# Eight value tiles of a two-layer trunk move into paired products, and the last projection leads with two tiles

## The chip, the cores and the metric

The kernel runs on one NeuronCore of one Trainium2 chip. The metric is the device time in microseconds of one execution. Three runs of the kernel before gave 2314.68, 2317.88 and 2318.4 us.

## The reference, cut to what matters

The reference is one inference step of a two-layer trunk over 512 sample tokens and 128 prompt tokens (640 columns, NT) with model width 2048. Layer 1, the odd one, has two mixers. Mixer C is differential attention: four heads, each with two query and two key maps of width 128 and one value of width 256. Mixer D is plain grouped attention with eight query heads and two key/value heads.

```python
cq, ck, cv, cg, dq, dk, dv, dg = split_cols(h @ w_in, ODD_SPLIT)
cv = cv.reshape(b, t, C_HEADS, C_V_DIM).transpose(0, 2, 1, 3)
...
o1 = attend(cq[:, 0][:, :, None], ck_all[:, 0], cv_all)[:, :, 0]
o2 = attend(cq[:, 1][:, :, None], ck_all[:, 1], cv_all)[:, :, 0]
o_c = rms_norm(o1 - lam.astype(o1.dtype) * o2, c_on) * (1.0 - lam_init)
y_c = o_c.transpose(0, 2, 1, 3).reshape(b, t, C_W) * jax.nn.silu(cg)
```

The branch outputs go through one output projection `w_out` and are added, gated, to the input of the layer. The gates of the conditioning come from `silu(c) @ ada_w`. The values of the prompt tokens are also an output (`new_c_v`).

## The kernel before, in words

**Tiles and products.** All activations lie with the 2048 features on 16 row blocks (k) of 128 partitions, 640 token columns each, and every one is split into a high and a low part (`split`, L240: ScalarE writes the high part, VectorE the difference), and so is every 128x512 quarter of weights (`split_w`, L260). A product is three matmuls: high by high, high by low, low by high. One output tile of 128 columns takes 16 blocks x 2 token halves of 320 x 3 = 96 matmuls (`proj_q`, L269). Weights come from DRAM over SP's queue into four `raw` buffers, up to five quarters ahead.

**Single tiles and pairs.** `run_tiles` (L312) computes tiles one by one, four quarters each. After each quarter `slot` (L301) advances the generators that wait in `prep` (the work on a finished tile, such as norms and transposes) and in `attn` (attention, one call per step) and the filler. Some first tiles, the leads, are computed together while their inputs are being made, so that each input serves several tiles. `run_pairs` (L435) computes two tiles from seven products instead of eight, each over 8 row blocks and one half of the tokens, with sums of weights made by VectorE (L467 to L477) and sums of activations made by `forms` (L1061). `project` (L1114) strings these together: three leads, singles up to n0, then pairs.

**Order.** The program's text gives the order in which work is emitted. The framework then orders instructions on each engine, so matmuls of attention can stand in the middle of a projection's quarter. Each engine, and SP's and GpSimd's DMA queues, work in the order so fixed.

**Layer 1's stages.** First the gates (L1430): 14 gate tiles, six as singles and eight as four pairs; each goes to DRAM (`gate_out`, L1396). Then the pool of buffers "mid" is closed, "odd" opened, and 38 single tiles run (L1484): for D query, key and value tiles (`q_gen` L625, `k_gen` L578, `v_gen` L672), then for each C head two query, two key and two value tiles, at the end two late gates (`very_late_gate`, L1445). `v_gen` copies the tile out of PSUM (`stage`, L554), transposes it to token rows in five blocks (`to_rows`, L560), splits it into `vh` and `vl`, and appends the attention of the head to `attn`. `diff_gen` (L1316) is the attention of one C head in 13 calls; `k_gen` drains `attn` before it overwrites a key buffer (L612). Between these runs the conditioning of layer 1 on VectorE (`ada_on_dve`, L191): four blocks of 32 steps of two products each (L213) and one closing step, at a rate FILL1 per quarter from quarter FILL1_FROM on.

**The end.** After the tiles `prep` and `attn` are drained (L1486, L1487), and layer 1's output projection begins with three leads whose inputs `y1_maker` (L1490) loads from DRAM in the order of quarters 0, 2, 3, 1: four tiles of a quarter through buffers "P" (L1502) or, in the other two quarters, three buffers "xr" (`late_yin`, L1102). At the ninth input the pool "odd" is closed and "fin" opened. The third lead accumulates in the PSUM tile that otherwise holds attention scores (`new_pp`, L280).

Of the kernel before, what the change touches and what calls it, by code (L numbers as in the profile page):

```python
# [11 lines left out]
F32 = mybir.dt.float32  # L12
# [36 lines left out]
FILL1 = 1.0  # L49
FILL1_FROM = 16  # L50
# [3 lines left out]
def trunk_kernel(ctx: ExitStack, tc: tile.TileContext, I: dict, O: dict):  # L54
# [523 lines left out]
    def k_gen(ap, pp, tag, src, gain, new_out):  # L578
        raw = ap.tile([P, 2, P], F32, tag="ctxk", name="ctxk", bufs=1)
        nc.sync.dma_start(raw, src.rearrange("(c p) d -> p c d", p=P))  # L580
        x = stage(ap, pp)
        yield
# [3 lines left out]
        for sample in (True, False):  # L586
# [35 lines left out]
        split(hi[:, CTX + NS:CTX + NT], lo[:, CTX + NS:CTX + NT], t)  # L622

# [48 lines left out]
    def v_gen(ap, pp, src, new_out, w=P, j=0, then=None):  # L672
        x = stage(ap, pp)
        yield
        if j == 0:
            drain(attn)
            st["v"] = tuple(ap.tile([P, 7, w], F32R, tag=t, name=t) for t in ("vh", "vl"))
            ctx_v(ap, src, *st["v"], w)
        hi, lo = st["v"]
        cols = slice(j * P, (j + 1) * P)  # L680
        t = to_rows(cols_of(x), True)
        split(hi[:, 2:6, cols], lo[:, 2:6, cols], t.rearrange("p (b f) -> p b f", b=4))
# [3 lines left out]
        split(hi[:, 6, cols], lo[:, 6, cols], vp)  # L686
# [144 lines left out]
    xdram, hdram, gdram = ([dram.tile([P, NT], F32, name=f"{n}{k}") for k in range(KT)] for n in ("xd", "hd", "gd"))  # L831
# [95 lines left out]
    def k_job(tag, src, gain, new_out):  # L927
        return lambda pp: k_gen(pools["cur"], pp, tag, src, gains[gain], new_out)
# [185 lines left out]
    def project(w, cols, n0, maker, job, begin, part, done, tail, **kw):  # L1114

        go_on = run_tiles([(cols[n], job(n)) for n in range(3)], w, maker, **{"order": (0, 2, 1, 3), **kw})


        quarters = [(cols[n], qd) for n in range(3, n0) for qd in range(4)]
# [10 lines left out]
        for n in range(3, n0):  # L1130
            pp, t = new_pp((n - 3) % 2), 4 * (n - 3)
# [298 lines left out]
    project(I["od_w_in"][0], [(OD["cg"] + i * P) if i < 8 else OD["dg"] + (i - 8) * P for i in FRONT], N_FRONT, h1_maker,  # L1430
# [31 lines left out]
    for n in range(4):  # L1462
# [4 lines left out]
        if n % 2 == 0:  # L1467
            jobs.append((OD["dk"] + kv * P, k_job(f"k{kv}", I["cache_d_k"][0, 0, kv], "d_k_norm", O["new_d_k"][0, 0, kv])))
            jobs.append((OD["dv"] + kv * P, v_job(I["cache_d_v"][0, 0, kv], O["new_d_v"][0, 0, kv], P, 0, then)))
# [116 lines left out]
```

## Time and profile before

| | |
|---|---|
| median of three runs | 2317.88 us (2314.68 to 2318.4) |
| profiled execution | 2318.59 us |
| its span, first to last instruction | 2316.8 us |
| mean granted TensorE clock | 0.997 |
| busy: TensorE, VectorE, ScalarE, GpSimd | 98%, 71%, 42%, 8% of the span |
| matmuls | 15892 |
| DMA | 342.94 MB, 148 GB/s over the span |

Layer 1's pairs run from about 1215 to 1317 us of the span, the odd stage to about 2088, the leads of the last projection to about 2137. The profile lists for each engine its busy time, for groups of instructions the count and mean duration and what ended the idle time before them, and in the windows view the busy time of each engine within a stretch. A matmul's listed duration includes its way through the array and overlaps the next one.

### The profile page before, as it was taken

What the parts mean: (1) busy time and instruction counts of PE and PEld (TensorE: products, weight loads), DVE (VectorE), ACT (ScalarE), POOL (GpSimd) and SP (SyncE); (2) the same over time, 40 slices, a digit from 0 to 9 for tenths busy, and PEclk for the clock granted to TensorE, in tenths of its full rate; (3) what the DMA queues carried; (4) which work ended last, traced back from release to release, by engine and by line L of the source; (5) the groups of instructions that cost most, each with busy time, mean ns of one, the idle gap of its engine ahead of it and who ended that gap; (6) DMA issues with size and microseconds to landing.
All of it is one profiled execution on the core that took longest, in us unless ns stands there. A gap on an engine that the chain in (4) does not pass through costs nothing.

```text
span 2316.8 us, 41604 instructions
## 1 busy us (share of the span) xinstructions
PE 2272.1 (98%) x15892; PEld 2197.3 (95%) x15892; DVE 1635.5 (71%) x3308; ACT 969.7 (42%) x2007; POOL 175.6 (8%) x243
## 2 busy tenths in 40 slices
PE   7999999999999999999999999999999999999999
PEld 5699999999999999999999999999999999999999
DVE  4559886786866663988887658659657658557576
ACT  4335442433422222544644445555453444434343
POOL 2111000000000000000100000000001010100101
PEclk9999999999999999999999999999999999999999
DMA  9874545445455543844773433224315233318532
GB/s 364 330 260 130 154 124 163 144 122 165 121 180 160 152 139 114 283 140 127 242 223 107 135 102 97 63 81 131 97 52 153 66 92 113 92 60 281 176 119 70
DMA packets 388456, 342.94 MB, mean 148 GB/s; under 512 B 19298, under 2 KB 327024, under 8 KB 387744
## 3 DMA queue, kind: packets, MB, share of 16 engines
q1 hardware_dynamic: 376000, 294.35, 41.9%
q0 software_dynamic: 11536, 43.77, 5.0%
q8 instruction: 125, 2.05, 0.4%
q10 hardware_dynamic: 720, 2.16, 0.3%
q14 instruction: 75, 0.61, 0.1%
HBM read 301.93 MB, written 38.28 MB: 147 GB/s over the span
## 4 chain that ended last, share of the span: by engine, by line
PE 86%; DVE 4%; ACT 3%; DMA 3%; issue 2%; POOL 1%; SPq 0%; ACTq 0%; POOLq 0%; DVEq 0%
PE pa L276 9%; PE pb L277 9%; PE pb L276 9%; PE pa L277 9%; PE pb L278 9%; PE pa L278 9%; PE pq L535 5%; PE pq L537 5%; PE pq L536 5%; PE T L715 2%; PE T L178 1%; PE S L727 1%; PE S L729 1%; PE S L728 1%; DMA yin<-yd 1%
## 5 line engine op out<-in xcount | busy, mean ns | idle before, releaser
L241 ACT ACTIVATE wh<-raw 128x512 fp32r<-128x512 f32 (+1 forms) x466 | 288.4, 619 | 723.8 <-PE pb L277 615.4
L276 PE MATMUL pa<-h,wh 128*128 128x320 f32 x1632 | 519.2, 319 | 4.8 <-ACT h L908 2.5
L242 DVE TENSOR_TENSOR wl<-raw,wh 128x512 fp32r<-128x512 f32 (+1 forms) x466 | 313.8, 674 | 296.3 <-ACT wh L241 260.9
L277 PE MATMUL pa<-h,wh 128*128 128x320 f32 x1632 | 508.3, 312 | 2.8 <-DVE h L242 2.7
L278 PE MATMUL pa<-h,wl 128*128 128x320 f32 x1632 | 506.9, 311 | 0.0
L278 PE MATMUL pb<-h,wl 128*128 128x320 f32 x1632 | 505.5, 310 | 0.0
L276 PE MATMUL pb<-h,wh 128*128 128x320 f32 x1632 | 505.2, 310 | 0.0
L277 PE MATMUL pb<-h,wh 128*128 128x320 f32 x1632 | 505.0, 309 | 0.0
L213 DVE SCALAR_TENSOR_TENSOR acc<-adaw,sT,acc 128x512 f32<-128x512 f32 (+1 forms) x600 | 358.3, 636 | 14.0 <-DMA adaw<-in_ada_w 13.7
L276 PEld LDWEIGHTS pa<-h,wh 128*128 128x128 f32 x1632 | 307.9, 189 | 18.2 <-issue 9.3
L277 PEld LDWEIGHTS pa<-h,wh 128*128 128x128 f32 x1632 | 308.4, 189 | 7.3 <-DVE h L242 4.5
L278 PEld LDWEIGHTS pa<-h,wl 128*128 128x128 f32 x1632 | 307.9, 189 | 3.3 <-issue 3.3
L278 PEld LDWEIGHTS pb<-h,wl 128*128 128x128 f32 x1632 | 306.6, 188 | 2.1 <-issue 2.1
L276 PEld LDWEIGHTS pb<-h,wh 128*128 128x128 f32 x1632 | 306.7, 188 | 0.0
L277 PEld LDWEIGHTS pb<-h,wh 128*128 128x128 f32 x1632 | 306.5, 188 | 0.1
L535 PE MATMUL pq<-h,wh 128*128 128x320 f32 x480 | 149.7, 312 | 0.4 <-DVE xr L1099 0.2
L536 PE MATMUL pq<-h,wh 128*128 128x320 f32 x480 | 148.4, 309 | 0.0
L537 PE MATMUL pq<-h,wl 128*128 128x320 f32 x480 | 148.0, 309 | 0.0
L701 ACT ACTIVATE p<-S,nm,rq 128x768 f32<-128x768 f32 (+3 forms) x120 | 101.2, 843 | 101.4 <-DVE nm L696 67.1
L535 PE MATMUL pq<-T,wh 128*128 128x320 f32 x360 | 111.2, 309 | 0.0
L536 PE MATMUL pq<-T,wh 128*128 128x320 f32 x360 | 111.2, 309 | 0.0
L537 PE MATMUL pq<-T,wl 128*128 128x320 f32 x360 | 111.2, 309 | 0.0
(326 smaller groups left out, 3699.8 us busy)
## 6 DMA issues: line engine op xcount, KB each, us to landing
adaw<-in_ada_w SPq DMA_DIRECT2D x192, 256.0 KB, 3.0
raw<-in_ev_w_in SPq DMA_DIRECT2D x184, 256.0 KB, 3.0
raw<-in_od_w_in SPq DMA_DIRECT2D x184, 256.0 KB, 2.9
ada<-in_ada_w SPq DMA_DIRECT2D x14, 2048.0 KB, 10.5
adaw<-in_ada_w SPq DMA_DIRECT2D x128, 128.0 KB, 2.2
yd<-y POOLq DMA_DIRECT2D x32, 320.0 KB, 3.0
yin<-yd SPq DMA_DIRECT2D x32, 320.0 KB, 4.4
w<-yd SPq DMA_DIRECT2D x32, 320.0 KB, 4.1
```

Source lines behind the costliest of these rows:

```text
L178: PE.matmul(acc[32 * g:32 * g + 32, 0:wd], sT[:, kt, :], w[:, kt % m, :], start=(i < 4), stop=(i >= KT - 4), tile_position=(0, 32 * g))
L213: V.scalar_tensor_tensor(out=a, in0=w, scalar=sT[:, kt, c:c + 1], in1=a, op0=ALU.mult, op1=ALU.add)
L241: A.activation(hi, x, AF.Copy)
L242: V.tensor_sub(lo, x, hi)
L276: PE.matmul(ps, wh[:, i, :], hi[:, sl], start=(j == js[0] if alone else (pos == 0 and j == 0)), stop=False)
L277: PE.matmul(ps, wh[:, i, :], lo[:, sl], start=False, stop=False)
L278: PE.matmul(ps, wl[:, i, :], hi[:, sl], start=False, stop=(j == js[1] - 1 if alone else (pos == 3 and j == 3)))
L535: PE.matmul(ps, wh[:, j, :], hi, start=(h == 0 and j == 0), stop=False)
L536: PE.matmul(ps, wh[:, j, :], lo, start=False, stop=False)
L537: PE.matmul(ps, wl[:, j, :], hi, start=False, stop=(h == 1 and j == 3))
L701: A.activation(p[:, 0:n], s, AF.Exp, scale=rsc, bias=nm, accum_out=l)
L715: PE.transpose(t[:, i * P:(i + 1) * P], p, ident)
```

## The change

The eight value tiles of mixer C leave the single tiles of the odd stage and follow the gates as four more pairs. `value_out` copies a finished half into the tile that the gates use for their tanh; `value_rows` transposes the finished tile to token rows, copies them, stores them to DRAM (`vdram`) and stores the prompt rows to the output. The first key tile of each head (`k_gen` with `vals`) loads its two value tiles back through buffers "stg" and splits them into `vh` and `vl`; the second one (`then`) appends the head's attention. In the odd stage the conditioning runs at 1.25 steps per quarter from the first quarter on, and attention at 1.1 calls per quarter from the fourteenth tile on. The drain of `attn` ahead of the last projection goes; that projection takes two leads instead of three (`n_lead`), and its inputs of the quarters 0 and 2 come through buffers "rp" and "stg" instead of "P".

```diff
-FILL1 = 1.0
-FILL1_FROM = 16
+FILL1 = 1.25
+FILL1_FROM = 0
...
-    def k_gen(ap, pp, tag, src, gain, new_out):
+    def k_gen(ap, pp, tag, src, gain, new_out, vals=None, then=None):
+        vx = []
+        def v_in(j):
+            vx.append(ap.tile([P, 5, P], F32, tag="stg", name="vx", bufs=2))
+            nc.sync.dma_start(vx[j].rearrange("p b f -> p (b f)"), vals[1][j])
...
         x = stage(ap, pp)
+        if vals:
+            v_in(0)
         yield
...
+        if vals:
+            v_in(1)
...
         split(hi[:, CTX + NS:CTX + NT], lo[:, CTX + NS:CTX + NT], t)
+        if vals:
+            yield
+            hi, lo = st["v"] = tuple(ap.tile([P, 7, 2 * P], F32R, tag=t, name=t) for t in ("vh", "vl"))
+            ctx_v(ap, vals[0], hi, lo, 2 * P)
+            for j in range(2):
+                cols = slice(j * P, (j + 1) * P)
+                split(hi[:, 2:7, cols], lo[:, 2:7, cols], vx[j])
+        if then:
+            attn.append(then())
...
-    def project(w, cols, n0, maker, job, begin, part, done, tail, **kw):
-        go_on = run_tiles([(cols[n], job(n)) for n in range(3)], w, maker, **{"order": (0, 2, 1, 3), **kw})
-        quarters = [(cols[n], qd) for n in range(3, n0) for qd in range(4)]
+    def project(w, cols, n0, maker, job, begin, part, done, tail, n_lead=3, **kw):
+        go_on = run_tiles([(cols[n], job(n)) for n in range(n_lead)], w, maker, **{"order": (0, 2, 1, 3), **kw})
+        quarters = [(cols[n], qd) for n in range(n_lead, n0) for qd in range(4)]
...
+    def value_rows(n, t):
+        yield
+        r = pools["cur"].tile([P, 5, P], F32, tag="xr", name="vr", bufs=3)
+        A.copy(r[:, 0:4, :], to_rows(cols_of(st[t]), True).rearrange("p (b f) -> p b f", b=4))
+        A.copy(r[:, 4, :], to_rows(cols_of(st[t]), False))
+        nc.gpsimd.dma_start(vdram[n], r.rearrange("p b f -> p (b f)"))
+        nc.gpsimd.dma_start(O["new_c_v"][0, 0, n // 2][:, n % 2 * P:(n % 2 + 1) * P], r[:, 4, :])
+    def value_out(n):
+        def put(t, sl, src):
+            A.copy(st[t][:, sl], src)
+            if (n, "v") in half_done:
+                prep.append(value_rows(n, t))
+            half_done.add((n, "v"))
+        return put
...
     def front_begin(p):
         for t in range(2):
-            outs[t] = gate_out(N_FRONT + 2 * p + t)
+            n = N_FRONT + 2 * p + t
+            outs[t] = gate_out(n) if n < len(FRONT) else value_out(n - len(FRONT))
...
-    project(I["od_w_in"][0], [(OD["cg"] + i * P) if i < 8 else OD["dg"] + (i - 8) * P for i in FRONT], N_FRONT, h1_maker,
+    project(I["od_w_in"][0], [(OD["cg"] + i * P) if i < 8 else OD["dg"] + (i - 8) * P for i in FRONT]
+            + [OD["cv"] + i * P for i in range(8)], N_FRONT, h1_maker,
             front_job, front_begin, None, front_done, front_tail, by_half=True)
...
         for m in range(2):
+            more = (None, diff_then(h)) if m else ((I["cache_c_v"][0, 0, h], vdram[2 * h:2 * h + 2]),)
             jobs.append((OD["ck"] + (m * 4 + h) * P,
-                         k_job(f"k{m}", I["cache_c_k"][0, 0, m, h], "c_k_norm", O["new_c_k"][0, 0, m, h])))
-        for j in range(2):
-            jobs.append((OD["cv"] + h * 256 + j * P,
-                         v_job(I["cache_c_v"][0, 0, h], O["new_c_v"][0, 0, h][:, j * P:(j + 1) * P], 256, j,
-                               diff_then(h) if j else None)))
-    brisk = {len(jobs), len(jobs) + 1}
+                         k_job(f"k{m}", I["cache_c_k"][0, 0, m, h], "c_k_norm", O["new_c_k"][0, 0, m, h], *more)))
+    brisk = {len(jobs): 1.5, len(jobs) + 1: 1.5}
+    brisk.update((i, 1.1) for i in range(13, len(jobs)))
...
     drain(prep)
-    drain(attn)
...
-            t = pools["cur"].tile([P, 768], F32, tag="P", name="yin", bufs=P_BUFS)[:, 0:NT]
+            tag, n = (("rp", 3), ("stg", 2))[k % 2]
+            t = pools["cur"].tile([P, NT], F32, tag=tag, name="yin", bufs=n)
...
-    project_out(1, y1_maker, rows_out, rows_last, lambda name: None, order=(0, 2, 3, 1))
+    project_out(1, y1_maker, rows_out, rows_last, lambda name: None, n_lead=2, order=(0, 2, 3, 1))
```

More of the change, by code (lines that the diff above doesn't have):

```diff
@@ L670, in ctx_v, with v_gen @@
         split(hi[:, 0:2, :], lo[:, 0:2, :], raw)
-    def v_gen(ap, pp, src, new_out, w=P, j=0, then=None):
+    def v_gen(ap, pp, src, new_out, then=None):
         x = stage(ap, pp)
         yield
-        if j == 0:
-            drain(attn)
[L677 to L680, printed above, removed]
+        drain(attn)
+        hi, lo = st["v"] = tuple(ap.tile([P, 7, P], F32R, tag=t, name=t) for t in ("vh", "vl"))
+        ctx_v(ap, src, hi, lo, P)
         t = to_rows(cols_of(x), True)
-        split(hi[:, 2:6, cols], lo[:, 2:6, cols], t.rearrange("p (b f) -> p b f", b=4))
+        split(hi[:, 2:6, :], lo[:, 2:6, :], t.rearrange("p (b f) -> p b f", b=4))
         t = to_rows(cols_of(x), False)
@@ L1129, in project @@
         go_on()
[L1130 to L1131 removed]
+        for n in range(n_lead, n0):
+            pp, t = new_pp((n - n_lead) % 2), 4 * (n - n_lead)
             for hv in ([HV] if n < n0 - 1 else [HV[1:], HV[:1]]):
```

14 lines of the change are left out of this document (7 added, 7 removed).

## The prediction

> **What bounds the kernel now.** I read the busy line of the page first, then the windows view by stage, then the groups of the stages that the change touches, and last the waits around two joins.
>
> ```profile
> span 2316.8 us, 41604 instructions
> ...
> PE 2272.1 (98%) x15892; PEld 2197.3 (95%) x15892; DVE 1635.5 (71%) x3308; ACT 969.7 (42%) x2007; POOL 175.6 (8%) x243
> ```
>
> TensorE (PE) is busy for 2272.1 of 2316.8 us, so all its idle time together is 44.7 us: a change gains by taking matmuls away, and loses by opening gaps. In the windows the first number after the stretch is its length, then come the busy time and instruction count of PE, weight loads, DVE, ACT and POOL, the granted clock, the DMA share and GB/s.
>
> ```profile
> 1215.00:1317.00 102.00, 102.00 (x696) 101.80 (x696) 77.30 (x128) 47.85 (x86) 4.41 (x9) 1.00 0.33 103
> 1317.00:1655.00 338.00, 334.95 (x2370) 324.80 (x2369) 239.36 (x537) 172.03 (x364) 26.10 (x27) 1.00 0.33 99
> 1655.00:2088.00 433.00, 424.24 (x2958) 412.60 (x2957) 276.39 (x637) 190.60 (x456) 42.06 (x54) 1.00 0.31 93
> 2089.00:2137.00 48.00, 45.21 (x300) 43.55 (x299) 37.80 (x68) 23.54 (x37) 2.77 (x4) 1.00 0.88 283
> ```
>
> The rows are: the gates' four pairs; the odd stage while mixer D's attention runs, and while mixer C's does; and the three leading tiles of layer 1's output projection. The pairs have no PE gap at all; D's stretch idles 3.0 us, C's 8.8, the lead 2.8. A matmul's listed 310 ns overlaps its neighbour, so its price is the distance between starts:
>
> ```profile
> 1240.10 0.31 PE L536 MATMUL pq<-h,wh 128*128 128x320 f32 x1
> ...
> 1241.42 0.31 PE L536 MATMUL pq<-h,wh 128*128 128x320 f32 x1
> ```
>
> These starts are nine matmuls and 1.32 us apart, and 102.00 us over 696 gives the same: **146.6 ns each**.
>
> **The change, part by part.**
>
> *Matmuls.* A single tile takes 16 row blocks x 2 halves x 3 products = 96 matmuls, two tiles 192. A pair takes 7 products of 8 x 3 = 24, so 168. Eight value tiles lose 768 from the C stage and put 672 into the front: 96 fewer, 96 x 146.6 ns = **-14.1 us**. The five transposes of a value tile move from its single tile to value_rows, count unchanged: nothing, between -0.5 and +1.
>
> *The load of a value pair on DVE and ACT.* Two single tiles need 8 weight splits, a pair 14, and the adds on top. (Groups: line, engine, operation, tiles, count, then busy us and mean ns of one, then the idle time before and its releaser.)
>
> ```profile
> L242 DVE TENSOR_TENSOR wl<-sx,wh 128x512 fp32r<-128x512 f32 x24 | 16.5, 688 | 12.2 <-ACT wh L241 12.2
> L470 DVE TENSOR_TENSOR sx<-sx,w 128x1024 f32<-128x1024 f32 x4 | 4.9, 1226 | 0.1
> L1400 DVE SCALAR_TENSOR_TENSOR g<-sq,tables 128x320 f32<-128x320 f32 x8 | 3.9, 487 | 0.0
> ```
>
> In the gates' pairs DVE has 77.30 us in 102.00, or 18.6 us in the 24.6 us that 168 matmuls take. A value pair replaces four gate products of 0.487 us by copies on ACT, so DVE falls to about 16.7 us. ACT, at 47.85 us there, gets four copies and two row copies in place of four tanh. PE hides all this as it does today: nothing. If that cover were gone a pair would last as long as its DVE work, which is still shorter. POOL issues two DMAs per tile instead of one; in that stage it is busy 4.41 of 102 us and nothing urgent queues behind them.
>
> *The end of the front.* The last value tile's transposes stand behind the last product, its add and its copy, and the front now ends by draining them, with the odd stage's first matmuls behind them on PE. An operation on 128x320 is 0.49 us (last row above) and the copy is near that, so the chain costs between 0 (PE gets odd-stage matmuls first) and 2.5 us. I take **+1**, two such operations.
>
> *Mixers D and C with fewer quarters.* The odd stage falls from 152 quarters to 120. By their matmuls the stretches hold:
>
> ```profile
> L276 PE MATMUL pa<-h,wh 128*128 128x320 f32 x352 | 112.5, 320 | 0.0
> L213 DVE SCALAR_TENSOR_TENSOR acc<-adaw,sT,acc 128x256 f32<-128x256 f32 x23 | 9.5, 479 | 0.5 <-DMA adaw<-in_ada_w 0.5
> ```
>
> The first row is one of six such groups of C's stretch: 2112 matmuls, 22 tiles, 88 quarters, so D's stretch has 64; all 32 quarters that go are C's. The conditioning needs 132 steps (four blocks of 33), each two of the second row. Before, it starts after 16 quarters and D takes 48; at 1.25 from the first quarter D takes 80, and C's 52 end well inside its 56 quarters. So 32 x 0.96 = 31 us of DVE move from C to D: D rises from 239.4 to 270 of 338 us (80%), C falls to 276.4 - 31 - 32 splits x 0.69 = 223 us in 433 - 768 x 0.1466 = 320 us (70%). The pairs run without a gap at 76%.
>
> The attention gets denser. One head of C is 13 calls. It enters in the third quarter of the next head's first tile and must be done by the third quarter of its second key tile: 12 quarters x 1.1 = 13.2 calls, so it just fits and the drain ahead of the key finds at most one. The waits that hurt C today are these:
>
> ```profile
> L1368 PE MATMUL T<-ident,on 128*128 128x128 f32 x36 | 7.5, 291 | 5.4 <-DVE on L1362 4.7 <-DVE kg L591 0.3
> L564 PE MATMUL T<-ident,m 128*128 128x128 f32 x28 | 4.9, 300 | 2.6 <-DVE m L609 2.4
> 2039.00:2089.00 50.00, 48.85 (x341) 46.46 (x340) 33.10 (x80) 21.38 (x49) 3.35 (x6) 1.00 0.23 69
> ```
>
> 8.0 us over four heads. The last row is the stretch that already runs 1.5 calls per quarter: it idles 1.15 of 50 us, 2.3%; 2.3% of 320 is 7.4 us, not more than today's 8.8. Against that stands the denser conditioning in D. Bounds: -3 (waits shrink with the stage) and +8 (they double). I take **+1**.
>
> Two value loads per head join SP's queue. They wait for stg buffers, the second one for the key tile's transposes; weight loads and the cache load queue behind them. Weights are loaded up to five quarters, 5 x 24 x 0.1466 = 17.6 us, ahead: nothing, and the same +8 if the cover goes.
>
> *The lead of the last projection.* Three leading tiles become two, the drain ahead of them goes, and the last head's calls 10 to 13 run inside the lead. PE's work there: 192 x 0.1466 = 28.1 us, and about 40 attention matmuls. In C, the 2958 - 2112 = 846 other matmuls share 424.24 - 2112 x 0.1466 = 115 us, 0.136 us each, so 5.4 us. Together 33.5 us, in which all 16 input tiles must be loaded and split.
>
> ```profile
> L241 ACT ACTIVATE h<-yin x16: 718/738/742, 2089.5 to 2126.0; 128x640 fp32r<-128x640 f32 x16
> DMA to landing us min/median/max: 2.7/4.3/6.1
> 2093.34 0.81 DVE L1455 TENSOR_TENSOR gg<-yg,gg 128x640 f32<-128x640 f32 x1
> ```
>
> Before, the 16 splits run from 2089.5 to 2126.0, 36.5 us, while PE has 48 us. The new buffers are tighter: the third and fourth input take buffers that the last gate (L1445) holds until its product, which today is over at 2094.15, some 5 us into the lead, and SP is held behind them. A load then takes 4.3 us to land. At the old pace the last input is split after 36.5 us and its 12 matmuls end about 1.8 us later: 38.3 us, 4.8 us idle where it was 2.8: +2. The early hold can add a short stall, so I take **+3**, between -2.8 (no idle left) and +21 (worked out below). That the third tile becomes a single one costs nothing: its 96 matmuls move.
>
> A longer stall costs more than its length:
>
> ```profile
> PE T L564 <- DVE m L609: 3.6, 4, 2.1
> 1778.00:1784.00 6.00, 4.79 (x34) 4.55 (x32) 4.91 (x12) 1.54 (x3) 1.88 (x2) 1.00 0.38 107
> 1784.00:1788.00 4.00, 3.09 (x13) 3.05 (x14) 3.57 (x8) 0.60 (x1) 0.00 (x0) 0.63 0.54 163
> 1788.00:1792.00 4.00, 4.00 (x28) 4.00 (x27) 2.94 (x8) 1.65 (x4) 0.00 (x0) 0.95 0.47 131
> ```
>
> In the waits (total, times, longest) the longest of this group is 2.1 us: 1.21 idle before 1784 and 0.91 after it. The stretch in which it ends has a clock of 0.63 and holds 13 matmuls where the next holds 28, so it loses 15 x 0.1466 = 2.2 us: 0.91 by idling, 1.3 by the clock.
>
> By the Trainium skill ("TensorE: Matmul & The Clock Gate", section "What's actually happening") the clock goes to half after at least one idle window of about 3.4 us and comes back after about 3.4 us of sustained work. The row differs: here a wait of 2.1 us was enough. By the page's figure no stall that I expect reaches the gate, and the lead's +3 would stay as it is; by the row a single 2 us stall makes it 3 + 1.3 = +4.3.
>
> *Sum.* -14.1 + 1 + 1 + 3 = -9.1 us. The profiled execution took 2318.59 us (span 2316.8), 0.7 above the median of 2317.88. 2318.6 - 9.1 = **2309.5 us**.
>
> **The rivals.**
>
> *Full gain.* The lead fills its waits with attention and gate work, and C keeps fewer waits as it shortens: -14.1 and up to -1 more, 2303 to 2305. For it: 1.5 calls per quarter cost only 2.3% idle. Against it: 33.5 us of PE work against 36.5 us of splits.
>
> *Starved in every quarter, clock falling.* Each of the lead's four quarters waits 2 us for its inputs and loses 1.3 us more to the clock: 13.2 us where 2.8 idle now, +10.4; with +2 elsewhere 2318.6 - 14.1 + 12.4 = 2316.9, no difference. For it: the 2.1 us stall above, and the DMA share of 0.88 with three tiles. Against it: three 320 KB loads overlap today, 36.5 / 16 = 2.3 us apart. The Trainium skill's page named above would give this case only for waits of about 3.4 us.
>
> *Loads one at a time (slower).* If SP, held by each buffer in turn, never has two inputs in flight, the 14 inputs behind the first two come 4.3 us apart: 60 us against 33.5 of work, 26.7 idle for 2.8, and with some overlap of the last ones +21: 2318.6 - 14.1 + 2 + 21 = 2327.5. It decides once the lead loses 16.0 us more than today, with the loads some 3.7 us apart ((33.5 + 2.8 + 16.0) / 14). The three buffers of the later eight inputs speak against it.
>
> *It doesn't do what it says.* The value pairs run slower than PE's pace and eat the 3.5 us that each should save: about 2318. The pairs' row, 102.00 of 102.00, speaks against it.
>
> **How the numbers follow.** About 0.2%, 4.6 us, is what a measurement of this kernel can tell from no change: faster is below 2313.2, slower above 2322.5. Forecast, 2305 to 2313.2: 0.50. Full gain: 0.20. Starved: 0.17. Not as it says: 0.03. Slower: 0.10. So faster 0.70, same 0.20, slower 0.10. The range 2303 to 2320 takes in the full gain and most of the starved case; what it leaves out is the slower rival and the edges, under 0.2.
>
> **What would show it.** PE should run 15796 matmuls: 224 more in each of the pairs' three lines, 256 fewer in each of the single tiles' three. The value pairs should last 24.6 us each without a PE gap; C's stretch about 320 us with some 8 us idle; the lead about 38 us with 4 to 6 us idle, waiting for yin. A lead over 50 us or at a clock below 1.00, more than 16 us idle in C, or value pairs longer than 25 us would make the forecast wrong.

## The result: slower by 0.3%, and the profile after

The changed kernel takes 2324.39 us (median of 7 runs, 2321.26 to 2327.76), the kernel before beside it 2316.97 us (7 runs, 2314.68 to 2319.36). The ratio is 1.0032 (95% interval 1.0020 to 1.0043), where 0.996 was forecast. The profiled execution took 2321.26 us, the shortest of the seven, so it shows somewhat less of the loss than the median does.

The busy line and four stretches of the changed kernel: the eight pairs, D's stretch, C's, the lead of the last projection; the fifth is a piece of the lead.

```profile
span 2319.5 us, 41525 instructions
...
PE 2259.1 (97%) x15796; PEld 2182.4 (94%) x15796; DVE 1678.2 (72%) x3364; ACT 991.9 (43%) x2043; POOL 184.0 (8%) x251
```

```profile
1213.00:1414.00 201.00, 201.00 (x1380) 200.76 (x1379) 144.75 (x229) 95.26 (x174) 11.50 (x22) 1.00 0.34 107
1414.00:1752.00 338.00, 332.64 (x2349) 322.34 (x2348) 255.80 (x586) 170.45 (x362) 28.59 (x28) 0.99 0.37 111
1752.00:2075.00 323.00, 311.30 (x2171) 298.62 (x2171) 229.69 (x527) 163.61 (x402) 39.46 (x46) 1.00 0.31 95
2075.00:2127.00 52.00, 37.85 (x241) 35.25 (x241) 35.74 (x71) 22.07 (x40) 4.51 (x6) 0.93 0.67 219
2104.00:2108.00 4.00, 2.83 (x10) 2.71 (x11) 2.85 (x5) 2.21 (x3) 0.00 (x0) 0.50 0.75 272
```

The 96 matmuls are gone and the pairs have no gap, as forecast. D's stretch idles 5.4 us (3.0 before), C's 11.7 (8.8 before). The lead idles 14.2 of 52.0 us, and its clock is 0.93. The waits of TensorE within the lead, then the groups of the input tiles and SP's issues from 2086 to 2106 (start, duration, queue, line, count):

```profile
PE pa L276 <- ACT h L241: 12.6, 4, 8.4
PE T L564 <- DVE xr L1117: 1.3, 1, 1.3
```

```profile
L241 ACT ACTIVATE h<-yin x16: 722/736/742, 2072.9 to 2121.4; 128x640 fp32r<-128x640 f32 x16
...
DMA to landing us min/median/max: 2.8/4.9/6.6
```

```profile
2088.67 9.58 SPq L254 DMA_DIRECT2D raw<-in_od_w_out  x4
2098.34 1.49 SPq L1122 DMA_DIRECT2D yin<-yd  x3
```

```profile
2096.41 0.38 PE L1386 MATMUL T<-ident,on 128*128 128x128 f32 x2
2105.17 0.64 PE L276 MATMUL pa<-h,wh 128*128 128x320 f32 x1 [8.37 <-ACT h L241]
2105.60 0.47 PE L276 MATMUL pb<-h,wh 128*128 128x320 f32 x1
2105.87 0.47 PE L276 MATMUL pa<-h,wh 128*128 128x320 f32 x1
```

Read them together. From 2088.67 on SP issues four weight loads that belong to the first *single* tile; each waits for a raw buffer, and they hold the queue for 9.58 us. Input 12 stands behind them: its load goes at 2098.34, and TensorE waits 8.37 us for its split. The 16 splits then take from 2072.9 to 2121.4, 48.5 us instead of 36.5.

All kernels below are divided in the same way, into five pieces of the span: the time up to the front's first pair matmul; the pairs; from there to the start of the last product of the late gates on VectorE (L1455 of the kernel before, inside the gates of L1445), the odd stage; from that product to the first pair matmul of the last projection, "lead and singles", which holds six tiles however many of them lead; the rest. Each number is the distance between two starts in the trace:

| | up to the pairs | pairs | odd stage | lead and singles | rest | span |
|---|---|---|---|---|---|---|
| before | 1216.0 | 98.6 | 778.7 | 88.9 | 134.5 | 2316.8 |
| after | 1213.2 | 201.0 | 660.4 | 110.7 | 134.1 | 2319.5 |
| three leads (e3_lead3) | 1215.0 | 201.0 | 666.9 | 93.2 | 134.3 | 2310.4 |
| two leads, three repairs (e18_bank_rawq) | 1214.8 | 201.0 | 662.9 | 99.5 | 134.7 | 2312.9 |
| best version (e15_best) | 1216.5 | 201.0 | 668.1 | 87.6 | 134.3 | 2307.4 |

Lead and singles grew by 21.8 us though the tiles are the same six. Two cautions go with the table. In the kernel before 14 matmuls of the lead start ahead of the dividing product, in the best version 13, in the other three kernels none; 14 x 0.1466 = 2.1 us. And each row is one execution: `e2_switch` and `e9_forms` below run the same instructions in the same order, and their lead and singles take 101.3 and 106.0 us, at a clock of 1.00 and 0.95. Their medians of ten differ by 0.4 us.

### The profile page after: what moved, and what is told of

Read it like the earlier page. It is cut to its first block, busy times and chain, and to the rows that moved or that the text cites. A ratio compares the mean times of both kernels' runs of the same rounds, so it can differ in the third digit from the quotient of the medians.

```text
span 2319.5 us, 41525 instructions
## 1 busy us (share of the span) xinstructions
PE 2259.1 (97%) x15796; PEld 2182.4 (94%) x15796; DVE 1678.2 (72%) x3364; ACT 991.9 (43%) x2043; POOL 184.0 (8%) x251
## 4 chain that ended last, share of the span: by engine, by line
PE 84%; DVE 6%; DMA 4%; ACT 2%; issue 2%; POOL 1%; SPq 0%; POOLq 0%; ACTq 0%; DVEq 0%
PE pa L276 8%; PE pb L277 8%; PE pa L277 8%; PE pb L276 8%; PE pa L278 8%; PE pb L278 8%; PE pq L535 7%; PE pq L536 7%; PE pq L537 7%; PE T L732 2%; DMA adaw<-in_ada_w 2%; DMA yin<-yd 1%; PE T L178 1%; PE S L744 1%; PE S L746 1%
## 5 line engine op out<-in xcount | busy, mean ns | idle before, releaser
L276 PE MATMUL pa<-h,wh 128*128 128x320 f32 x1520 | 483.8, 319 | 15.8 <-ACT h L241 13.3
L277 PE MATMUL pa<-h,wh 128*128 128x320 f32 x1520 | 474.0, 312 | 1.0 <-DVE h L242 0.6
L278 PE MATMUL pa<-h,wl 128*128 128x320 f32 x1520 | 472.4, 311 | 0.0
L278 PE MATMUL pb<-h,wl 128*128 128x320 f32 x1520 | 471.5, 310 | 0.0
L277 PE MATMUL pb<-h,wh 128*128 128x320 f32 x1520 | 471.0, 310 | 0.0
L276 PE MATMUL pb<-h,wh 128*128 128x320 f32 x1520 | 470.8, 310 | 0.0
L213 DVE SCALAR_TENSOR_TENSOR acc<-adaw,sT,acc 128x512 f32<-128x512 f32 (+1 forms) x600 | 359.4, 637 | 12.4 <-DMA adaw<-in_ada_w 11.9
L276 PEld LDWEIGHTS pa<-h,wh 128*128 128x128 f32 x1520 | 286.8, 189 | 29.3 <-ACT h L241 14.9
L277 PEld LDWEIGHTS pa<-h,wh 128*128 128x128 f32 x1520 | 286.9, 189 | 6.0 <-DVE h L242 2.9
L276 PEld LDWEIGHTS pb<-h,wh 128*128 128x128 f32 x1520 | 286.0, 188 | 0.4 <-issue 0.4
L277 PEld LDWEIGHTS pb<-h,wh 128*128 128x128 f32 x1520 | 285.9, 188 | 0.1
L535 PE MATMUL pq<-h,wh 128*128 128x320 f32 x608 | 189.7, 312 | 0.7 <-ACT wh L241 0.7
L536 PE MATMUL pq<-h,wh 128*128 128x320 f32 x608 | 187.9, 309 | 0.0
L537 PE MATMUL pq<-h,wl 128*128 128x320 f32 x608 | 187.8, 309 | 0.0
L535 PE MATMUL pq<-T,wh 128*128 128x320 f32 x456 | 140.9, 309 | 0.0
L537 PE MATMUL pq<-T,wl 128*128 128x320 f32 x456 | 140.9, 309 | 0.0
L536 PE MATMUL pq<-T,wh 128*128 128x320 f32 x456 | 140.9, 309 | 0.0
```

Of the source, the lines that this page charges most:

```text
L213: V.scalar_tensor_tensor(out=a, in0=w, scalar=sT[:, kt, c:c + 1], in1=a, op0=ALU.mult, op1=ALU.add)
L276: PE.matmul(ps, wh[:, i, :], hi[:, sl], start=(j == js[0] if alone else (pos == 0 and j == 0)), stop=False)
L277: PE.matmul(ps, wh[:, i, :], lo[:, sl], start=False, stop=False)
L278: PE.matmul(ps, wl[:, i, :], hi[:, sl], start=False, stop=(j == js[1] - 1 if alone else (pos == 3 and j == 3)))
L535: PE.matmul(ps, wh[:, j, :], hi, start=(h == 0 and j == 0), stop=False)
L536: PE.matmul(ps, wh[:, j, :], lo, start=False, stop=False)
```

## The experiments

### The lead: queue, pool switch, number of leads

The first theory was the order of SP's queue; the rival was that two leads have too little work for the inputs' supply. `e1_rawq` puts the four weight loads on GpSimd's queue:

```diff
-                raws.append(load_raw(w, *quarters[len(raws)]))
+                raws.append(load_raw(w, *quarters[len(raws)], queue=nc.gpsimd if n_lead == 2 and len(raws) < 4 else None))
```

> The changed kernel, but the four weight loads of the first single tile after the lead are issued on GpSimd's queue instead of SP's. Theory (queue order): in the changed kernel these four loads stand on SP ahead of the lead's ninth input and wait for weight buffers that TensorE frees only when it has finished the quarter at hand; off SP, the 8.6 us stall shrinks to 3 us or less and the time falls from 2324 to about 2315. Rival (supply): two leads use inputs faster than the loads and their buffers can bring them, whatever the queue order; the stall only moves, the time stays within 3 us of 2324. Rival (pool switch): the ninth input waits for buffers of the last attention calls; the stall stays at about 8 us, the time at 2324.

Measured: 2322.66 us (10 runs, 2315.47 to 2324.7), ratio to before 1.0017 (1.0007 to 1.0027). The waits of TensorE in its lead:

```profile
PE pa L276 <- ACT h L241: 5.3, 4, 2.0
PE T L564 <- DVE xr L1117: 1.3, 1, 1.3
```

The 8.4 us wait is gone, and the waits for inputs fall from 12.6 to 5.3 us, but the median gains only 1.7 us. So the weight loads on SP's queue made that one long wait, but it is not the whole price. `e2_switch` closes the pool "odd" and drains the attention at input 4, the last quarter, instead of input 12:

```diff
-        if k == 12:
+        if k == 4:
...
-        if k % 8 >= 4:
+        if 4 <= k < 8:
             late_yin(k)
```

> The changed kernel, but buffer pool 'odd' is closed and 'fin' opened one quarter later, at input 4 instead of input 12; inputs 12 to 15 come through 'rp' and 'stg' too. Theory (queue order): inputs 12 to 15 now stand ahead of the four weight loads, but inputs 4 to 7 stand behind them, so a stall of 4 to 8 us appears in the last quarter instead; 2319 to 2325. Rival (pool switch): nothing of the last quarter depends on attention any more, the stall goes altogether, about 2314. Rival (supply): unchanged, 2324.

Measured: 2318.3 us, ratio 1.0008 (0.9998 to 1.0017): 6.1 us of the loss come back. This edit also puts inputs 12 to 15 ahead of the four weight loads (issued from 2094.67 on, for 9.61 us), so it ends the 8.4 us wait too, and its 6.1 us overlap with the 1.7 us of `e1_rawq`. The 16 splits take 36.7 us again (2078.3 to 2115.0). `e3_lead3` goes back to three leads, with the attention drained ahead of them and the inputs in buffers "P", and gives the last head 2.25 calls per quarter:

```diff
-    brisk = {len(jobs): 1.5, len(jobs) + 1: 1.5}
+    brisk = {len(jobs): 2.25, len(jobs) + 1: 2.25}
...
     drain(prep)
+    drain(attn)
...
-            tag, n = (("rp", 3), ("stg", 2))[k % 2]
-            t = pools["cur"].tile([P, NT], F32, tag=tag, name="yin", bufs=n)
+            t = pools["cur"].tile([P, 768], F32, tag="P", name="yin", bufs=P_BUFS)[:, 0:NT]
...
-    project_out(1, y1_maker, rows_out, rows_last, lambda name: None, n_lead=2, order=(0, 2, 3, 1))
+    project_out(1, y1_maker, rows_out, rows_last, lambda name: None, order=(0, 2, 3, 1))
```

> The changed kernel with the lead of the kernel before: three leads, the drain of attention ahead of them, inputs through buffers 'P'; so that the drain finds little, attention runs 2.25 calls per quarter in the last two tiles. Theory (the lead costs it): the lead is back at 47 us with one tile more, the pairs' 14.1 us come out less some 5 us of waits in the odd stage: 2309 to 2313. Rival (the odd stage costs it): waits in mixers C and D eat the gain, and the lead's stall is only where it shows; 2320 or more.

Measured: 2312.53 us, ratio 0.9982 (0.9972 to 0.9991): faster than before. The rest of the change is a gain, and the new lead, with the last head's slower pace, turns it into a loss: 2324.4 - 2312.5 = 11.9 us. `e4_lead2_alone` is the other half: the kernel before with only the lead's part of the change.

```diff
-    drain(attn)
...
+            tag, n = (("rp", 3), ("stg", 2))[k % 2]
...
-    project_out(1, y1_maker, rows_out, rows_last, lambda name: None, order=(0, 2, 3, 1))
+    project_out(1, y1_maker, rows_out, rows_last, lambda name: None, n_lead=2, order=(0, 2, 3, 1))
```

> The kernel before with the lead part of the change alone: two leads, no drain ahead of them, inputs through 'rp' and 'stg'; the value tiles stay single tiles. Theory (queue order): here one weight load stands ahead of the ninth input, not four, and one attention call is left for the lead, not four; the stall stays under 3 us, 2317 to 2321. Rival (supply): two leads starve here too, with 10 us or more idle in the lead, 2326 to 2330.

Measured: 2325.22 us, ratio 1.0038 (1.0026 to 1.0050). Two leads cost 8 us on the kernel before too, where no 8 us wait shows. Lead and singles take 98.0 us instead of 88.9:

```profile
2089.00:2137.00 48.00, 43.22 (x253) 40.62 (x253) 36.49 (x64) 22.38 (x36) 5.37 (x8) 0.89 0.86 276
2089.00:2099.00 10.00, 8.50 (x36) 7.79 (x37) 7.79 (x14) 4.75 (x9) 2.77 (x4) 0.66 0.77 232
```

TensorE is busy 43.22 us here, yet starts 253 matmuls where the same 48 us held 300 before: a part of the loss is clock (0.89) and not waiting. In its first 10 us (second row) the clock is 0.66, though no wait there is longer than 0.85 us.

### What the two leads wait for

`e9_forms`, which stands on `e2_switch`, was to start the forms of the last projection (16 more loads of 320 KB, `w`) after the last input instead of at the switch.

```diff
-            attn.append(forms(ydram))
...
+        if k == 7:
+            attn.append(forms(ydram))
```

> The kernel with two leading tiles and the pool switch at input 4 (e2_switch, 2318.3 us), with the forms of the last projection (16 more loads of 320 KB) started after the last input instead of at the switch. Theory A (the inputs of the lead share the DMA engines, 0.8 to 0.9 busy there, with the forms' loads): the two late waits of the lead, 1.9 and 3.3 us, fall under 1 us each and the lead and the single tiles together fall from 101.3 to 96 us or so, 2312 to 2315. Theory B (the inputs wait for buffers and for the order of the sync queue): the waits stay, 2317 to 2319. If the forms, started later, hold up the pairs: slower than 2320.

Measured: 2317.91 us, ratio 1.0000 (0.9990 to 1.0009). No gain, but the edit moved nothing. The forms are advanced only after all four inputs of a quarter are in the program, so both texts give one order: on every engine and queue the trace has the same instructions in the same order as that of `e2_switch`. The forms' first two loads still stand ahead of the last input:

```profile
2103.77 1.05 SPq L1086 DMA_DIRECT2D w<-yd  x2
2109.38 0.32 SPq L1122 DMA_DIRECT2D yin<-yd  x1
2109.74 3.42 SPq L1086 DMA_DIRECT2D w<-yd  x4
```

So whether the forms' loads hold up the inputs stays untested. `e10_half` leaves out work: in `e4_lead2_alone` every second input is neither loaded nor split, and the one before it is used twice.

```diff
-        if k % 8 >= 4:
+        if k % 2:
+            hs[k] = hs[k - 1]
+        elif k % 8 >= 4:
```

> The kernel before with two leading tiles alone (e4_lead2_alone, 2325.22 us), in which every second input is neither loaded nor split: an odd input is the even one before it again, so half of the inputs' supply is left out and the matmuls are all there. Theory A (supply: 28 us of matmuls against inputs that come 2.3 us apart): the lead's waits vanish, lead and single tiles fall from 98.0 to about 88 us, as with three leading tiles, and the time to 2314 to 2317. Theory B (it is the attention calls, the buffers of the last gate or the weights): at least half of the 8 us stays, over 2320.

Measured: 2321.63 us, ratio 1.0015 (1.0006 to 1.0025), 3.6 us under `e4_lead2_alone` (5.3 us by the two ratios, 4.3 us in lead and singles): less than supply alone promised, more than nothing. The lead's largest waits in this run:

```profile
PE T L564 <- DVE xr L1099: 2.5, 2, 2.0
PE pa L277 <- DVE h L242: 1.5, 1, 1.5
```

The larger one is not for an input but for xr, the first lead's residual sum. It is 3.0 us in `e2_switch` (first row below), so `e11_later` moves the transposes that wait for it one quarter back (second row):

```diff
                 yield
+                if l and n < 2:
+                    yield
                 finish(n)
```

> The kernel with two leading tiles and the pool switch at input 4 (e2_switch, 2318.3 us), in which the two leading tiles' row transposes come one quarter later. Theory A (a third part of the lead's loss is the residual: its load waits for one of three buffers that the last inputs hold, is issued at 2116.2, lands 4.9 us later, and TensorE stands 3.3 us before the first transpose of the sum): the 3.3 us and its clock go, 2314 to 2316. Theory B (TensorE is behind the inputs anyway): the wait moves to the next input, 2317.5 to 2319.

```profile
PE T L564 <- DVE xr L1117: 3.0, 1, 3.0
```

```profile
PE pa L276 <- DVE xr L1117: 3.0, 1, 3.0
```

Measured: 2318.12 us, ratio 1.0001 (0.9992 to 1.0010). The wait kept its length and only changed the waiter: now the first single tile's projection (pa) waits for xr. Its PSUM tile is that of the first lead, which is free only when the residual (loaded late, through a buffer that the last inputs hold) has been added. With three leads two other leads' quarters, 2 x 24 x 0.1466 = 7.0 us, lie in between; with two leads one, 3.5 us. `e17_bank` gives the first single the third lead's PSUM tile, and `e18_bank_rawq` the queue of `e1_rawq` besides.

```diff
-            pp, t = new_pp((n - n_lead) % 2), 4 * (n - n_lead)
+            pp, t = new_pp((n - n_lead) % 2 if n_lead == 3 or n > n_lead else 2), 4 * (n - n_lead)
```

> The kernel with two leading tiles and the pool switch at input 4 (e2_switch, 2318.3 us), whose first single tile uses the PSUM bank that the third leading tile had, instead of the first leading tile's. Theory A (with two leading tiles only one tile's quarter, 24 x 0.1466 = 3.5 us, lies between the first leading tile's last matmul and the first single tile's first, which must wait until the residual has landed and the sum has read the bank; three leading tiles give 7 us): the 3.0 us that TensorE waits there go, 2314 to 2316. Theory B (TensorE would wait for the next input or weight anyway): 2317 to 2319.

> The same (e17_bank), with the first single tile's four weight loads on the GpSimd queue besides. If queue order, bank and switch are all that two leading tiles cost, 2311 to 2313.5, like three leading tiles; if the inputs' supply is the rest of it, 4 us or more stay: 2314 to 2317.

Measured: 2315.79 us, ratio 0.9995 (0.9986 to 1.0004), and 2315.91 us, ratio 0.9997 (0.9988 to 1.0006). In the profile of `e18_bank_rawq` no wait of the lead for xr is over 0.3 us:

```profile
PE pa L276 <- ACT h L241: 1.4, 2, 1.2
PE T L1386 <- DVE on L1380: 0.7, 1, 0.7
PE T L564 <- DVE xr L1117: 0.7, 2, 0.3
```

By the medians the PSUM tile ("bank") was worth 2.5 us, the queue then nothing more. The 2.5 us are near the noise: the intervals of `e2_switch` and `e17_bank` overlap, and the profiled execution of `e17_bank`, the second longest of its ten, has lead and singles at 102.0 us, no shorter than 101.3; there the longest wait for xr is 1.1 us instead of 3.0. Two leads with all three repairs stay 3.4 us behind three leads. `e12_early` asks the same from the other side: the kernel before with two leads, but with its own attention and buffers, and the transposes later.

```diff
+                if l and n < 2:
+                    yield
...
-    project_out(1, y1_maker, rows_out, rows_last, lambda name: None, order=(0, 2, 3, 1))
+    project_out(1, y1_maker, rows_out, rows_last, lambda name: None, n_lead=2, order=(0, 2, 3, 1))
```

> The kernel before with two leading tiles, but with the attention finished ahead of the lead and the inputs in the buffers that it had before, and with the row transposes one quarter later. Theory A (the 8 us that two leading tiles cost in e4_lead2_alone, 2325.22 us, are the early hold by the last gate's buffers with a clock of 0.66 after it, some 4 to 5 us, and the residual, 3 us): 2316 to 2319, within 0.1% of the kernel before. Theory B (supply of inputs against 28 us of matmuls): at least 5 of the 8 us stay, 2322 or more.

Measured: 2324.42 us, ratio 1.0028 (1.0016 to 1.0040). So theory A, that the early hold and the residual were the price of the 8 us, doesn't hold by the median. The edit moves the residual's wait, as in `e11_later`, and doesn't take it away. In the profiled execution lead and singles take 94.3 us, 3.7 less than in `e4_lead2_alone`; the median is 0.8 us less. Its lead's waits:

```profile
PE pa L276 <- ACT h L241: 3.6, 4, 2.1
PE pa L276 <- DVE xr L1099: 1.3, 1, 1.3
```

Inputs come first (3.6 us), the bank second (1.3 us).

### The odd stage: conditioning or attention

`e3_lead3` has the old lead and still stands above the forecast 2309.5. Its waits between 1420 and 2060 us, beside those of the kernel before:

```profile
PE T L1386 <- DVE on L1380: 7.3, 6, 2.2
PE T L564 <- DVE m L620: 5.3, 4, 3.0
```

```profile
PE T L1368 <- DVE on L1362: 4.2, 8, 0.8
PE T L564 <- DVE m L609: 2.4, 3, 2.1
```

The same two places, 6 us more. The edits below stand on `e3_lead3`. `e6_fill` thins the conditioning out:

```diff
-FILL1 = 1.25
+FILL1 = 1.125
```

> The kernel with three leading tiles (e3_lead3, 2312.53 us), with the conditioning at 1.125 steps per quarter instead of 1.25. Theory A (the conditioning is too dense in D's stretch: DVE stands 1.06 us for the key's r and up to 0.55 us at a time for adaw loads, so that the key's m is 3.3 us late at 1472, and 2.2 and 2.5 us are lost in the same way at 1862 and 1925): these three waits fall to under 1.5 us each, the odd stage falls from 666.9 to about 663 us and the time to about 2308.5 to 2310.5. Theory B (the odd stage's loss is the denser attention of C alone): the waits at 1472 and 1862 may move but the time stays at 2311.5 to 2313.5.

Measured: 2316.61 us, ratio 0.9998 (0.9987 to 1.0009). Slower than `e3_lead3`, which neither theory had; its profiled execution (2312.48 us) is the shortest of its ten, so the profile does not show why. `e7_out` moves the transposes of a finished row block behind the next scores:

```diff
-            if u >= 2:
-                out(u - 2)
             if u < 5:
                 score(u, 0)
             if 1 <= u < 6:
                 groups(u - 1)
+            if u >= 2:
+                out(u - 2)
```

> The kernel with three leading tiles (e3_lead3, 2312.53 us), with a C call's transposes of the finished row block (out) moved behind the scores and the probability transposes of the same call. Theory B (two calls in one quarter put out right behind weigh, and PE stands 1.76 us for the chain on, ssq, rn, on: at 1843, 1937 and 2024, and with 2.5 and 0.8 at 1925 and 1889): these waits fall under 0.8 us each, C's stretch loses 4 to 6 us and the time is 2306.5 to 2309. Theory A (the loss is the conditioning's): under 2 us, 2310.5 to 2312.5. That the wait only moves to the next instruction that needs on: no change, 2312.5.

Measured: 2311.64 us, ratio 0.9974 (0.9965 to 0.9984), not to be told from `e3_lead3`. The waits at 1843, 1935 and 2023 stay. VectorE and GpSimd ahead of the first of them:

```profile
1840.10 0.82 DVE L609 TENSOR_TENSOR kg<-kg,r 128x640 f32<-128x640 f32 x1 [1.35 <-POOL r L608]
1840.84 0.48 DVE L1373 TENSOR_SCALAR on<-T,rl 128x256 f32<-128x256 f32 x1
...
1842.51 0.15 DVE L1377 TENSOR_SCALAR ssq<-ssq 128x1 f32<-128x1 f32 x1
...
1844.32 0.48 DVE L1380 SCALAR_TENSOR_TENSOR on<-on,rn,con 128x256 f32<-128x256 f32 x1 [0.46 <-POOL rn L1379]
```

A head's last row block (on) stands on VectorE behind the next head's key (kg), which waits for GpSimd's r; then ssq stands behind that key's rotation, and rn goes through GpSimd again. `e14_fast` gives C's attention 1.3 calls per quarter, so that a head ends ahead of that key; `e13_quiet` leaves the conditioning out for two quarters behind each key:

```diff
-    brisk.update((i, 1.1) for i in range(13, len(jobs)))
+    brisk.update((i, 1.3) for i in range(13, len(jobs)))
```

> The kernel with three leading tiles (e3_lead3, 2312.53 us), with C's attention at 1.3 calls per quarter instead of 1.1. Theory A (the last two calls of a head meet the next head's first key on DVE and POOL: on stands behind kg, which waits for POOL's r, and rn behind that, so TensorE stands 1.76 us for on at 1843, 1937 and 2024; at 1.3 the head is done in 10 quarters, ahead of that key): these three go, 2307 to 2309.5. Theory B (more calls per quarter make other waits for on, as 2.5 us at 1925): no gain or a loss, 2312 to 2316.

```diff
-FILL1 = 1.25
+FILL1 = 1.36
...
-                slot(fill, rate if t > fill_from else 0.0, steps(i))
+                slot(fill, rate if t > fill_from and not (quiet(i) and qd < 2) else 0.0, steps(i))
```

> The kernel with three leading tiles (e3_lead3, 2312.53 us), with no conditioning step in the two quarters behind a key tile and 1.36 steps in the others. Theory A (the key's preparation on DVE stands behind conditioning steps whose loads are late): the waits of 3.3 us at 1472 and 2.2 us at 1862 fall under 1 us and the odd stage from 666.9 to 662 or so, 2307 to 2309. Theory B (as dense as that the steps hold something else up, or the wait is the chain through POOL): a gain under 2 us, 2310.5 to 2313.

Measured: `e14_fast` 2313.01 us, ratio 0.9978 (0.9969 to 0.9988): the three waits went, and others of 0.7 to 2.5 us came at the keys and at on in their place. `e13_quiet` 2312.5 us, ratio 0.9975 (0.9965 to 0.9985): its odd stage is 662.8 us, 4.1 shorter, and its lead and singles 97.7 us, 4.5 longer, with a wait of 2.9 us for the last head's final on ahead of the lead. The wait at 1862 went; the one at the first key, its other target, stayed at 2.9 us, and conditioning steps still run between that key's operations on VectorE (at 1472.12 and 1474.40). `e16_end` takes only the last head faster, and `e15_best` puts this together with the edits of `e13_quiet` and `e7_out`:

```diff
-    brisk = {len(jobs): 2.25, len(jobs) + 1: 2.25}
+    brisk = {len(jobs): 2.75, len(jobs) + 1: 2.75}
```

> The kernel with three leading tiles (e3_lead3, 2312.53 us), with the last head's attention at 2.75 calls per quarter instead of 2.25, nothing else. Theory A (the drain ahead of the lead costs 2.1 and 0.9 us and its clock there): 2309 to 2311. Theory B (the calls only wait earlier): 2312 to 2314.

> The kernel with no conditioning step behind a key tile (e13_quiet, 2312.5 us), with C's out behind the scores and with the last head's attention at 2.75 calls per quarter instead of 2.25. Theory A (e13 shortened the odd stage by 4 us and lost it again because the last head's final call stood 3.2 us for on ahead of the lead): that wait falls under 1 us and both gains add up, 2307 to 2310. Theory B (the odd stage and the lead share one supply, so that what the one saves the other waits for): 2311 to 2313.5.

Measured: `e16_end` 2312.63 us, ratio 0.9981 (0.9971 to 0.9991), no gain. This edit moved nothing either: the trace has the same instructions in the same order on every engine as `e3_lead3`, so it says nothing on the last head's pace. `e15_best` 2307.51 us (5 runs, 2306.14 to 2313.09), ratio 0.9964 (0.9950 to 0.9977): faster than both kernels. Its lead:

```profile
2085.00:2133.00 48.00, 47.12 (x318) 45.97 (x318) 39.27 (x70) 22.30 (x34) 3.92 (x6) 1.00 0.91 299
```

It idles 0.9 us and runs at full clock; the window of the kernel before held 300 matmuls, this one 318. The gain over `e3_lead3` lies in lead and singles (87.6 against 93.2 us; 25 matmuls that started in it stand ahead of the dividing product), and not in a shorter odd stage (668.1 against 666.9). `e7_out` alone has the same 25 matmuls ahead of it and 88.9 us in lead and singles. The first key's wait is 3.5 us here.

Last, the wait of 3.0 us at the odd stage's first key (first row, `e3_lead3`; before has none there). `e20_from14` starts the conditioning behind that key (second row), `e19_best14` does so in the best version:

```diff
-FILL1 = 1.25
-FILL1_FROM = 0
+FILL1 = 1.28
+FILL1_FROM = 14
```

> The kernel with three leading tiles (e3_lead3, 2312.53 us), with the conditioning started after 14 quarters, behind the first key's preparation, at 1.28 steps per quarter. Theory A (the early start costs the 3.3 us at 1472 and some 1.5 us of clock): this wait vanishes, as in the kernel before, and the odd stage falls from 666.9 by about 4 us: 2308 to 2310. Theory B (a wait of that kind falls on some key wherever the conditioning runs): another key waits 2 to 3 us more, and the time is 2311 to 2314.

> The best version (e15_best, 2307.51 us), with the conditioning started after 14 quarters at 1.55 steps per quarter. Theory A: the 3.8 us at 1474 and the clock behind it go, 2302.5 to 2305. Theory B: at 1.55 the steps make as much waiting at later keys, 2306 to 2309.

```profile
PE T L564 <- DVE m L620: 3.0, 1, 3.0
```

```profile
PE T L564 <- DVE k0l L242: 1.0, 1, 1.0
```

Measured: 2312.82 us, ratio 0.9976 (0.9966 to 0.9985), and 2307.58 us, ratio 0.9961 (0.9948 to 0.9973). The early start does cause that wait, and taking it away buys no time: in `e20_from14` the odd stage is 3.7 us shorter than in `e3_lead3`, lead and singles 2.7 us longer.

## Why the prediction was wrong, point by point

**Matmuls: right.** 15796 were run, and the pairs' 201.00 us have no gap. Four more pairs add 102.4 us to the front: four of 24.6 make 98.4, and the other 4 us are 35 transposes that the odd stage no longer has. The +1 for the end of the front did not come: the odd stage's first projection matmul starts 0.28 us after the last pair matmul (1414.25 to 1414.53).

**The lead: the step that failed.** "Together 33.5 us, in which all 16 input tiles must be loaded and split ... so I take +3." Lead and singles grew by 21.8 us. 2.1 of them are the 14 matmuls that started ahead of the dividing product before; 5.4 us of attention that was to move there and the 3 forecast make 8.4 more, so this term is 11.3 us too small. TensorE idles 14.1 us in this piece where it idled 2.2, at a clock of 0.97 where it was 1.00. (The other differences between the two profiled executions add up to 0.5: front and odd stage together lost 3.7 us more than forecast, and 3.2 us less went by before the pairs and after the lead.) The forecast kept the old pace of the splits, 36.5 us; it was 48.5. That pace was not a property of the loads. In the kernel before three weight loads stand ahead of input 12 and hold the queue for 4.12 us (from 2097.28 on); now four hold it for 9.58. Four things made the loss, by the medians:

- The pool switch with its drain in the middle of the lead, 6.1 us (`e2_switch`), the long wait of the third point among them. I had put the end of the attention into the lead as work that fills waits. That the switch, and the inputs behind it, had to wait for that attention is argued from the program; `e2_switch` moves the switch and the place of the weight loads together.
- The first single tile's PSUM tile, 2.5 us, near the noise (`e17_bank`): "That the third tile becomes a single one costs nothing: its 96 matmuls move." Its matmuls were the cover for the first lead's residual.
- Weight loads ahead of input 12 on SP, the one wait of 8.4 us. It was 1.7 us of the median when repaired alone and nothing after the two repairs above, so its own share stays open.
- What is left to three leads, 3.4 us, probably from supply: with half of the inputs left out two leads gained 3.6 us (`e10_half`). Other edits differ between those two kernels, the last head's pace among them, and the forms' loads were not tested, so this share is argued and not isolated. It is close to the forecast: with all three repairs (`e18_bank_rawq`) the splits take 37.0 us and lead and singles idle 4.4 us, where 36.5 and 4.8 were forecast. The sum was right for a lead whose pace holds; what it left out were the switch, the queue and the third tile's cover.

The clock belongs to it: the long wait left 0.50 behind it for some 4 us. The rival "starved in every quarter" named the right kind of loss, waits and clock, at 10.4 us against some 14 (the 11.3 and the 3); the rival "loads one at a time" came nearest to the time (2327.5), but its mechanism did not occur: the inputs were held at one place, not in turn.

**D and C: mis-sized.** I took +1 with bounds of -3 and +8. The two stretches' idle time rose from 11.8 to 17.1 us, 5.3 us. Where the attention is not moved into the lead (`e3_lead3`), front and odd stage gave 102.4 - 111.8 = -9.4 us where -14.1 + 2 = -12.1 was forecast. Even this flatters them, since 26 matmuls more than before (615 against 589) start in its lead and singles. With that piece the sum is 961.1 - 966.2 = -5.1 us, so some 9 of the 14.1 us were lost where the forecast let 2 go. In the odd stage and the lead together TensorE idles 20.1 us in `e3_lead3` and 14.6 before. VectorE's load was near the forecast: 255.8 and 229.7 us in the two stretches, where 270 and 223 were worked out. The row that I scaled from, 1.5 calls per quarter at 2.3% idle, was the stretch of the last head, with no next key to meet. That waits come from meetings on VectorE and GpSimd is shown by the rows of `e7_out` for three of them and by `e20_from14` for the first key; that thinning the conditioning did not help (`e6_fill`) stays open.

**No single wait was found that carries the odd stage's loss.** Three edits took waits away and gained nothing by the medians (`e13_quiet`, `e14_fast`, `e20_from14`), each within an interval of some 2 us to either side. In the profiled executions the first and the last of them gave back in lead and singles what the odd stage saved, by 2.7 to 4.5 us, which is no more than two executions of one program differ there (4.7 us). The three edits of `e15_best` together gained 5.0 us over `e3_lead3`, and their intervals overlap slightly. Of the three, `e7_out` gained 0.9 us alone, `e13_quiet` none, and the pace of `e16_end` changed no order when it stood alone. Why they gain more together is not shown.

**The clock.** The row at 1784 had a 2.1 us wait cost 1.3 us more by the clock; the +3 left that out. The lead of `e4_lead2_alone` shows that such waits do count: no wait over 2.8 us, a clock of 0.89, and 0.66 in ten of these us with no wait over 0.85. By the Trainium skill ("TensorE: Matmul & The Clock Gate", section "What's actually happening") half clock follows on idle windows of about 3.4 us and full clock on about 3.4 us of work; the 8.4 us wait agrees with both (0.50, then matmul starts 0.267 us apart until 2108.87), the shorter waits do not, and here the measurement decides.

## What to carry to other kernels

A lead that makes its inputs while it works is a pipeline of queue, buffers and PSUM: before its work is cut, ask of each input what stands ahead of its load in the issuing queue, and of each output tile what it covers. A pace measured in one arrangement holds only while that arrangement's cover stands. When several waits are near the same size, judge them together before calling any of them free: none of the three edits of the best version gave over 1 us alone, and together they gave 5. And an edit of the program's text is a change only if the trace shows another order of instructions: two of the edits here gave the same order, and their times say nothing about the theories that they were made for.

## What the runs showed of the hardware

After the 8.37 us wait TensorE started 13 matmuls in 3.7 us (2105.17 to 2108.87), most of them 0.267 us apart against 0.147 before, in a stretch whose granted clock is 0.50: that stop cost 3.7 - 13 x 0.147 = 1.8 us beyond its length. On SP's DMA queue four loads that waited for buffers took 9.58 us to issue, and held up the inputs behind them, whose own latency was 2.8 to 6.6 us; with the four on GpSimd's queue (`e1_rawq`) the 8.4 us wait was gone.
